# Two delays in the hand-written weaving of a recurrence: the first half starts nearer the head of the products, its first steps lie closer

## The chip, the cores and the metric

The kernel runs on one core of one Trainium2 chip. The metric is the device time of one execution in microseconds, as the median of several runs. One execution was also profiled; the times "in the trace" are those of that one execution, counted from its start.

## The reference, cut to what matters

The program has two layers over 1024 tokens with a width of 2048 (16 heads of 128). Only layer one, a gated linear recurrence (HGRN2), is touched by the change:

```
q, fz, i, g = split(h @ w_in, 4)
logf = log(lb + (1 - lb) * sigmoid(fz));  k = (1 - lb) * sigmoid(-fz);  v = i
b = cumsum(logf)  (in chunks)
o_t = q_t . S_t,   S_t = diag(f_t) S_{t-1} + k_t^T v_t          (per head)
out = (rms(o) * silu(g)) @ w_out
```

The recurrence is done in chunks: inside a chunk as a small masked attention of `q*exp(b)` with `k*exp(-b)`, between chunks by a state of 128 x 128 per head. Layer two (attention with a forget gate) follows and stays as it was.

## The kernel before, in words

Layer one is worked off in eight pairs of heads (`p` = 0 to 7). Per pair there are four big products with float32 split into two parts (three matmuls for each piece of 128 rows, called a k below): `v` (`gemm_N`, moving tiles of 256 columns), `g`, then `f` and `q` (`gemm_T`, 512 columns, eight k of three matmuls, so 24 matmuls for one head and one token half). `f` and `q` run twice, for token half `th` = 0 and then `th` = 1: f of head j=0, f of j=1, q of j=0, q of j=1.

The recurrence of one half of one pair is a generator, `hg_half`. Its steps are `hg_att` for each head (scores on TensorE, masked on VectorE by L503, and the transposition of k, copied by ScalarE in L507), `hg_state` for both heads (products on TensorE, then the state chain on VectorE: L523 for the first chunk, L525 for three more), `hg_out` for each head (seven or eight fp32 products into the tile `oa`, then square L540, sum L542, an rsqrt in small steps L221 to L227, scaling L544), and `hg_turn` for each head (four transposes of the result, a copy L552, gate L553, stores of 64 KB through SP).

What each engine executes is fixed when the program is built. The order on TensorE is written by class `Weave`: it chains all matmuls in the order in which Python emits them. `Weave` keeps a clock of its own, which only counts: `PE.tick(0.65)` after each k of a `gemm_T` and 0.33 after a k of `gemm_N`. A generator that was spawned with a delay takes its next step at the first tick after it is due; the number that it yields is the delay to its next step. `PE.need(mark)` forces steps out early when later code depends on them. The order on the other engines follows from the order in which the operations are recorded, with a scheduler that may move them.

The forget gate `hg_forget` runs for each head and half as soon as its f product is done. On ScalarE it needs a table load and two sigmoids (L470, L471), a table load and a logarithm (L472), and, after VectorE has made a running sum (L473) and small columns from it (L479 to L483), a table load and exponentials (L487, `dl` in L484, L485, L486). GpSimd scales k (L474). The decay column `dl` is kept in a dictionary that the state step reads when it is recorded:

```
        u["dl"] = dl                                            # end of hg_forget
...
        kT, st, dl = c128(u["kT"]), c128(u["S"]), u["dl"]       # hg_state
...
                    V.scalar_tensor_tensor(st[:, (n + 1) % 4, :], st[:, n, :], dl[:, 4 + n:5 + n],
                                           pu[:, n * P:(n + 1) * P], ALU.mult, ALU.add)
```

So the state steps L525 of a head use the `dl` of whichever forget gate of that head was recorded last before them.

The split of the next pair's weights into two parts (`split_w`: the high part by ScalarE in L232, the rest by GpSimd in L233, two pieces of 128x1024 each) lies in the same stretch: once between f and q of the second half (next `v` weights) and once after q (next `g` weights).

Of the kernel before, what the change touches and what calls it, by code (L numbers as in the profile page):

```python
# [82 lines left out]
def hybrid_trunk_kernel(ctx: ExitStack, tc: tile.TileContext, x, c, mod_w, mod_b, norm_g, a_w_in,  # L83
# [4 lines left out]
    PE = Weave(tc, nc.tensor)  # L88
# [32 lines left out]
    def ar(b, off, n, dt=F32):  # L121

        return pr(place.get(b, b), off, n, dt)
# [4 lines left out]
    def mm_ps():  # L128
        return psp.tile([P, 512], F32, tag="mm", name="mm", bufs=3)
# [118 lines left out]
    def raw_next():  # L248

        while not raws["ready"]:  # L250
            raw_load()
        return raws["ready"].pop(0)
# [12 lines left out]
    def mod_sum(*todo):  # L265

        for rb, acc in todo:
            V.tensor_scalar(acc, rawk(rb, 0), csil[:, 0:1], None, ALU.mult)
        for k in range(1, KT):
            for rb, acc in todo:  # L270
                V.scalar_tensor_tensor(acc, rawk(rb, k), csil[:, k:k + 1], acc, ALU.mult, ALU.add)  # L271
# [18 lines left out]
    def split_w(eng=None, more=True):  # L290

        rb = raw_next()
        i = wn[0] % 2
        wn[0] += 1
        for q in range(2):
            halves(eng or G, ar(8 + 2 * i, 1024 * q, 1024, F32R), ar(9 + 2 * i, 1024 * q, 1024, F32R),
                   ar(rb, 1024 * q, 1024))
        if more:
            raw_load()
        return (lambda k: ar(8 + 2 * i, k * 256, 256, F32R)), (lambda k: ar(9 + 2 * i, k * 256, 256, F32R))  # L300
# [8 lines left out]
    def gemm_T(ps, w, j, th):  # L309

        for k in range(KT):
            gemm_Tk(ps, w, j, th, k)
            PE.tick(0.65)
# [8 lines left out]
    def gemm_N(ps, w, t):  # L322

        for u in range(2):
            for k in range(KT):
                gemm_Nk(ps[:, u * 256:(u + 1) * 256], w, t + u, k)
                PE.tick(0.33)
# [165 lines left out]
    def hg_att(j):  # L493

        u = us[j]
        pa, pk = c128(sm_ps()), sm_ps()
        ks, qd, kst = c128(u["ks"]), c128(u["qd"]), c128(u["kst"])
        for n in range(4):
            PE.matmul(pa[0:64, n, :], lhsT=ks[:, n, 0:64], rhs=qd[:, n, :], start=True, stop=True)
            PE.matmul(pa[64:P, n, 64:P], lhsT=ks[:, n, 64:P], rhs=qd[:, n, 64:P], start=True, stop=True)  # L500
        for rows, cs in ((slice(0, 64), slice(0, P)), (slice(64, P), slice(64, P))):
            m = keep[rows, cs]
            V.copy_predicated(u["att"][rows, :, cs],  # L503
                              m.rearrange("p (o q) -> p o q", o=1).broadcast_to([64, 4, m.shape[1]]), pa[rows, :, cs])
        for n in range(4):
            PE.transpose(pk[:, n * P:(n + 1) * P], kst[:, n, :], ident)
        S.activation(u["kT"], pk, AF.Copy)  # L507

    def hg_state(j, th, v):

        u = us[j]
        pu = sm_ps()
        kT, st, dl = c128(u["kT"]), c128(u["S"]), u["dl"]
        js = slice(j * P, (j + 1) * P)
        nl = 3 if th == 1 else 4
        for n in range(nl):
            PE.matmul(pu[:, n * P:(n + 1) * P], lhsT=kT[:, n, :], rhs=v(th * 4 + n)[:, js], start=True, stop=True)
        with tc.high_priority():
            if th == 1:
                V.tensor_scalar(st[:, 0, :], st[:, 0, :], dl[:, 0:1], None, ALU.mult)  # L520
            for n in range(nl):
                if th == 0 and n == 0:
                    V.tensor_copy(st[:, 1, :], pu[:, 0:P])  # L523
                else:
                    V.scalar_tensor_tensor(st[:, (n + 1) % 4, :], st[:, n, :], dl[:, 4 + n:5 + n],  # L525
                                           pu[:, n * P:(n + 1) * P], ALU.mult, ALU.add)

    def hg_out(h, j, th, v):
        u = us[j]
        po = oa_ps()  # L530
        pov = c128(po)
        att, qd, st = u["att"], c128(u["qd"]), c128(u["S"])
        js = slice(j * P, (j + 1) * P)
        for n in range(4):
            first = th == 0 and n == 0
            PE.matmul(pov[:, n, :], lhsT=att[:, n, :], rhs=v(th * 4 + n)[:, js], start=True, stop=first)
            if not first:
                PE.matmul(pov[:, n, :], lhsT=qd[:, n, :], rhs=st[:, n, :], start=False, stop=True)
        sq = u["sq"]
        S.activation(sq, po, AF.Square)  # L540
        ss = sml.tile([P, 4], F32, name="ss")
        V.tensor_reduce(ss, c128(sq), AX.X, ALU.add)  # L542
        r = rsqrt_mean(ss, 4, 1.0 / P)
        V.tensor_tensor(c128(sq), pov, spread(r, 4, P), ALU.mult)  # L544

    def hg_turn(h, j, th, sg):

        u = us[j]
        pg = sm_ps()
        for n in range(4):  # L550
            PE.transpose(pg[:, n * P:(n + 1) * P], u["sq"][:, n * P:(n + 1) * P], ident)
        S.activation(u["ogT"], pg, AF.Copy, scale=ongc[:, h:h + 1])  # L552
        G.tensor_tensor(u["ogT"], u["ogT"], sg(j, th), ALU.mult)  # L553
        for n in range(4):
            dma(ogd[th * 4 + n][:, h, :], u["ogT"][:, n * P:(n + 1) * P])

    def hg_half(p, th, v, sg):
        for j in range(2):
            hg_att(j)
            PE.marks.add(("att", p, j, th))  # L560
            yield 4.5
        if p > 0 or th == 1:
            PE.need(("out", p - 1 + th, 1, 1 - th))
        for j in range(2):
            hg_state(j, th, v)
        yield 4.0
        if p > 0 or th == 1:
            PE.need(("half", p - 1 + th, 1 - th))
        for j in range(2):
            hg_out(2 * p + j, j, th, v)  # L570
            PE.marks.add(("out", p, j, th))
            yield 5.0
        yield 2.0
        for j in range(2):
            hg_turn(2 * p + j, j, th, sg)
            yield 3.0
        PE.marks.add(("half", p, th))

    def hg_pair(p, wv, wg):
        bv, bg = 14 + (p % 2) * 2, 15 + (p % 2) * 2  # L580

        def v(t):
            return ar(bv, t * 256, 256)

        def sg(j, th):
            return ar(bg, j * 1024 + th * 512, 512)

        def put_v(ps, t):
            S.activation(ar(bv, t * 256, 512), ps, AF.Copy)

        def put_g(ps, j, th):
            S.activation(sg(j, th), ps, AF.Sigmoid)
            V.tensor_tensor(sg(j, th), ps, sg(j, th), ALU.mult)

        if p == 0:
            for t in range(0, NT, 2):
                put_v(vps[t // 2], t)
            for j in range(2):
                put_g(gps[j], j, 0)
        else:  # L600
            for t in range(0, NT, 2):
                ps = mm_ps()
                gemm_N(ps, wv, t)
                put_v(ps, t)
        wf = split_w()
        for th in range(1 if p == 0 else 0, 2):
            for j in range(2):
                ps = mm_ps()
                gemm_T(ps, wg, j, th)
                put_g(ps, j, th)  # L610
        wq = split_w()

        for i in range(3):
            mod_sum((raw_next(), accs[i]))
            raw_load()
            PE.spawn(mod_later(mods_left.pop(0), accs[i]), 15.0 + 5.0 * i)
        for th in range(2):
            if th == 1:
                PE.spawn(hg_half(p, 0, v, sg), 5.0)
            for j in range(2):  # L620
                ps = mm_ps()
                gemm_T(ps, wf, j, th)
                if p > 0 or th == 1:
                    PE.need(("att", p - 1 + th, j, 1 - th))
                hg_forget(2 * p + j, us[j], ps)
            if th == 1:
                nwv = split_w() if p + 1 < NP else None
            for j in range(2):
                ps = mm_ps()
                gemm_T(ps, wq, j, th)  # L630
                if p > 0 or th == 1:
                    PE.need(("out", p - 1 + th, j, 1 - th))
                V.tensor_tensor(us[j]["qd"], ps, us[j]["eb"], ALU.mult)
        nwg = split_w() if p + 1 < NP else None
        PE.spawn(hg_half(p, 1, v, sg), 5.0)
        return nwv, nwg

    def mod_later(b, acc):
        mod_cols(b, acc, sm_ps()[:, 0:256])
        PE.marks.add(("mod", b))  # L640
        yield 0.0

    for p in range(NP):
        wv, wg = hg_pair(p, wv, wg)
# [737 lines left out]
```

## Time and profile before

| | |
|---|---|
| median of 3 runs | 2374.51 us (2373.2 to 2376.35) |
| profiled execution, its own time | 2370.9 us |
| its span in the trace | 2369.2 us |
| TensorE (PE) busy | 2263.2 us, 96% |
| VectorE (DVE) / ScalarE (ACT) / GpSimd (POOL) busy | 63% / 43% / 25% |

How to read it: PE is busy nearly all the time, so the time can only fall where PE is idle or runs at the lower clock, and it rises where a new idle stretch opens on PE. Idle time of the other engines costs nothing by itself.

### The profile page before, as it was taken

How to read it: one execution, taken by the hardware profiler on the slowest of the kernel's cores; microseconds unless marked ns; L12 is line 12 of the kernel's file. 1: busy time of each engine (PE TensorE's matmuls, PEld its weight loads, DVE VectorE, ACT ScalarE, POOL GpSimd, SP SyncE). 2: the span in 40 equal slices, each digit the busy share in tenths (PEclk: the TensorE clock that was granted, in tenths of full speed). 3: DMA queues.
4: the chain of work that ended last, by engine and by line, in shares of the span. 5: the costliest groups of instructions: out<-in, count | busy, mean ns of one | idle time of the engine just before them, and what ended most of it. 6: DMA issues, size and time to landing. Idle time of an engine off the chain costs nothing.

```text
span 2369.2 us, 38021 instructions
## 1 busy us (share of the span) xinstructions
PE 2263.2 (96%) x14376; PEld 2026.4 (86%) x14376; DVE 1501.3 (63%) x3838; ACT 1016.6 (43%) x1634; POOL 601.9 (25%) x514
## 2 busy tenths in 40 slices
PE   4999999999999999999798999999999999999999
PEld 3888888888888798788688999989999999998887
DVE  7565555665656566646867547667767766777533
ACT  5454444444353536324323324444544544455321
POOL 3222222221222221101332222433343334333000
PEclk9999999999999999999899999999999999999999
DMA  8313131313132223565322323512222222235443
GB/s 272 102 41 103 45 98 46 98 54 98 55 89 72 72 85 95 189 217 182 106 90 81 124 86 99 177 57 68 88 74 73 88 78 84 68 94 175 154 145 115
DMA packets 220315, 245.18 MB, mean 103 GB/s; under 512 B 14610, under 2 KB 182964, under 8 KB 220132
## 3 DMA queue, kind: packets, MB, share of 16 engines
q1 hardware_dynamic: 220132, 242.75, 32.8%
q8 instruction: 113, 1.85, 0.3%
q14 instruction: 70, 0.57, 0.1%
HBM read 196.36 MB, written 46.34 MB: 102 GB/s over the span
## 4 chain that ended last, share of the span: by engine, by line
PE 73%; DVE 11%; ACT 6%; issue 4%; DMA 4%; POOL 1%; SPq 0%; ACTq 0%; DVEq 0%; POOLq 0%
PE mm L48 53%; PE oa L48 8%; PE sm L48 7%; PE sm L51 5%; DVE blk L233 2%; DVE blk L271 1%; DVE dl L479 1%; ACT blk L232 1%; DVE blk L473 1%; ACT L472 1%; DMA blk<-in_mod_w_dram 1%; ACT L487 1%; ACT blk L472 1%; POOL blk L233 1%; ACT L470 1%
## 5 line engine op out<-in xcount | busy, mean ns | idle before, releaser
L48 PE MATMUL mm<-blk,blk 128*128 128x512 f32 (+1 forms) x9120 | 1726.0, 343 | 15.2 <-DVE blk L233 7.9
L48 PEld LDWEIGHTS mm<-blk,blk 128*128 128x128 f32 x9120 | 1419.5, 192 | 185.9 <-DVE blk L233 10.5
L232 ACT ACTIVATE blk<-blk 128x1024 fp32r<-128x1024 f32 (+3 forms) x372 | 335.4, 914 | 461.2 <-PE mm L48 281.1
L233 DVE TENSOR_TENSOR blk<-blk,blk 128x1024 fp32r<-128x1024 f32 (+3 forms) x268 | 276.2, 1039 | 228.8 <-ACT blk L232 225.2
L233 POOL TENSOR_TENSOR blk<-blk,blk 128x1024 fp32r<-128x1024 f32 (+1 forms) x104 | 240.0, 2314 | 308.6 <-ACT blk L232 302.5
L48 PE MATMUL oa<-blk,blk 128*128 128x256 f32 (+1 forms) x2016 | 286.4, 287 | 27.8 <-DVE blk L523 14.7
L48 PEld LDWEIGHTS oa<-blk,blk 128*128 128x128 f32 x2016 | 267.4, 196 | 39.2 <-DVE blk L523 16.0
L48 PE MATMUL sm<-blk,blk 128*128 128x256 f32 (+6 forms) x1824 | 269.2, 303 | 0.1
L48 PEld LDWEIGHTS sm<-blk,blk 128*128 128x128 f32 (+2 forms) x1824 | 218.2, 175 | 23.2 <-issue 3.5
L51 PE MATMUL sm<-ident,blk 128*128 128x128 f32 x1201 | 187.8, 277 | 36.2 <-DVE blk L931 12.6
L51 PEld LDWEIGHTS sm<-ident,blk 128*128 128x128 f32 x1201 | 144.6, 142 | 63.3 <-issue 32.0
L1226 ACT ACTIVATE blk<-blk,m 128x128 f32<-128x128 f32 (+7 forms) x128 | 99.0, 773 | 127.5 <-DVE m L1224 117.4
L233 DVE TENSOR_TENSOR blk<-sm,blk 128x512 fp32r<-128x512 f32 (+1 forms) x160 | 92.9, 581 | 62.7 <-ACT blk L232 62.2
L1228 POOL TENSOR_SCALAR blk<-blk,smx 128x128 f32<-128x128 f32 (+7 forms) x128 | 98.1, 767 | 135.6 <-DVE smx L1227 121.2
L271 DVE SCALAR_TENSOR_TENSOR blk<-blk,cc,blk 128x256 f32<-128x256 f32 x196 | 111.2, 570 | 20.6 <-DMA blk<-in_mod_w_dram 13.8
L1198 POOL TENSOR_TENSOR blk<-rows4k,keep 128x128 f32<-128x128 f32 x128 | 63.0, 492 | 226.8 <-DVE mx L1205 208.4
L553 POOL TENSOR_TENSOR blk<-blk,blk 128x512 f32<-128x512 f32 x32 | 42.5, 1327 | 238.4 <-ACT blk L552 238.4
L232 ACT ACTIVATE blk<-sm 128x512 fp32r<-128x512 f32 (+1 forms) x160 | 81.1, 507 | 48.7 <-PE sm L51 47.9
L1205 DVE CUSTOM_DVE_ANT_0 blk<-sm,rows4k 128x128 f32<-128x128 f32 (+3 forms) x176 | 84.6, 494 | 22.9 <-PE sm L48 21.4
L474 POOL TENSOR_SCALAR blk<-blk,cc 128x512 f32<-128x512 f32 x32 | 22.9, 716 | 260.7 <-ACT blk L471 257.4
L487 ACT ACT_TABLE_LOAD x31 | 39.8, 1283 | 103.0 <-DVE blk L482 103.0
L473 DVE TENSOR_TENSOR_SCAN blk<-rows4k,blk 128x512 f32<-128x512 f32 x32 | 39.1, 1223 | 70.3 <-ACT blk L472 70.3
(167 smaller groups left out, 1776.2 us busy)
## 6 DMA issues: line engine op xcount, KB each, us to landing
blk<-in_a_w_in_dram SPq DMA_DIRECT2D x64, 512.0 KB, 3.9
blk<-in_mod_w_dram SPq DMA_DIRECT2D x48, 512.0 KB, 4.7
blk<-in_kv_w_dram SPq DMA_DIRECT2D x32, 512.0 KB, 4.1
blk<-in_b_w_in_dram SPq DMA_DIRECT2D x32, 512.0 KB, 3.9
ogd<-blk SPq DMA_DIRECT2D x128, 64.0 KB, 1.9
blk<-in_kv_mod_w_dram SPq DMA_DIRECT2D x16, 512.0 KB, 3.5
blk<-in_a_w_out_dram SPq DMA_DIRECT2D x16, 512.0 KB, 3.9
blk<-ogd SPq DMA_DIRECT2D x16, 512.0 KB, 3.8
```

The costliest lines, as they stand in the source:

```text
L48: self._chain(self.PE.matmul(*a, **k))
L51: self._chain(self.PE.transpose(*a, **k))
L232: S.activation(hi, src, AF.Copy)
L233: eng.tensor_tensor(lo, src, hi.bitcast(F32), ALU.subtract)
L271: V.scalar_tensor_tensor(acc, rawk(rb, k), csil[:, k:k + 1], acc, ALU.mult, ALU.add)
L472: S.activation(u["lf"], u["lf"], AF.Ln, bias=lc, scale=oc)
L473: V.tensor_tensor_scan(u["b"], rst, u["lf"], 0.0, ALU.mult, ALU.add)
L487: S.activation(lf[:, :, 1, :], lf[:, :, 1, :], AF.Exp)
L1198: G.tensor_tensor(nfm, nF[:, i * P:n], negm, ALU.add)
L1205: V.tensor_tensor_reduce(dst, src, add, 1.0, -3e38, ALU.add, ALU.max, mx[:, nm:nm + 1])
L1226: S.activation(l[:, 0:n], l[:, 0:n], AF.Exp, bias=m, accum_out=sm)
L1228: G.tensor_scalar(l[:, 0:n], l[:, 0:n], sm, 0.0, ALU.mult, ALU.add)
```

## The change

Two numbers. The delay with which the first half's `hg_half` is spawned at the start of the second half's f product goes from 5.0 to 1.0, and the delay after each `hg_att` from 4.5 to 3.5 (that one holds for both halves of every pair).

```
@@ -558,7 +558,7 @@
         for j in range(2):
             hg_att(j)
             PE.marks.add(("att", p, j, th))
-            yield 4.5
+            yield 3.5
         if p > 0 or th == 1:
             PE.need(("out", p - 1 + th, 1, 1 - th))
         for j in range(2):
@@ -616,7 +616,7 @@
             PE.spawn(mod_later(mods_left.pop(0), accs[i]), 15.0 + 5.0 * i)
         for th in range(2):
             if th == 1:
-                PE.spawn(hg_half(p, 0, v, sg), 5.0)
+                PE.spawn(hg_half(p, 0, v, sg), 1.0)
             for j in range(2):
                 ps = mm_ps()
                 gemm_T(ps, wf, j, th)
```

The order on TensorE (PE), first pair, at the head of the second half's f product of head 0. The `mm` rows are that product, the `sm` rows with 64x128 and 64x64 are `hg_att` of head 0, L51 its transposes.

```order
 L48 MATMUL mm<-blk_0_77,blk_0_87 128x512
+L48 MATMUL sm<-blk_0_111,blk_0_109 64x128
+L48 MATMUL sm<-blk_0_111,blk_0_109 64x64
+L48 MATMUL sm<-blk_0_111,blk_0_109 64x128
+L48 MATMUL sm<-blk_0_111,blk_0_109 64x64
+L48 MATMUL sm<-blk_0_111,blk_0_109 64x128
+L48 MATMUL sm<-blk_0_111,blk_0_109 64x64
+L48 MATMUL sm<-blk_0_111,blk_0_109 64x128
+L48 MATMUL sm<-blk_0_111,blk_0_109 64x64
+L51 MATMUL sm<-ident,blk_1_110 128x128 x4
 L48 MATMUL mm<-blk_0_79,blk_0_85 128x512
 L48 MATMUL mm<-blk_1_80,blk_0_85 128x512
```

The step stands now behind 2 of the 8 k of that product; before it stood behind all 8. Counted on PE in the same way for every pair but the last (there the output projection follows in place of the next v product): `hg_att` of head 1 moves from behind 7 k of f of head 1 to behind 7 k of f of head 0; `hg_state` from behind 6 k of q of head 0 to behind 5 k of f of head 1; `hg_out` of head 0 from behind the whole of q of head 0 to behind its first 3 k; `hg_out` of head 1 from behind the whole of q of head 1 to behind its first 3 k; `hg_turn` of head 0 from behind 84 matmuls of the next pair's v product to behind 30, that of head 1 from behind 111 to behind 57.

The order on ScalarE (ACT), third pair, from behind the logarithm of head 0's second half to that of head 1. First before; the two L232 are the pieces of the next v weights, L484 is `dl`, L507 the copy of `hg_att` of head 1.

```order
L232 ACTIVATE blk_0_85<-blk_0_93 128x1024
L487 ACT_TABLE_LOAD
L487 ACTIVATE blk_0_105<-blk_0_105 128x4x64
L484 ACTIVATE dl<-dl 128x8
L485 ACTIVATE blk_1_108<-blk_0_107 128x512
L486 ACTIVATE blk_0_109<-blk_0_107 128x512
L507 ACTIVATE blk_0_113<-sm 128x512
L470 ACT_TABLE_LOAD
L470 ACTIVATE blk_0_105<-mm 128x512
L471 ACTIVATE blk_1_106<-mm 128x512
L472 ACT_TABLE_LOAD
L472 ACTIVATE blk_0_105<-blk_0_105,cc 128x512
```

And the same place of the changed kernel:

```order
L232 ACTIVATE blk_0_85<-blk_0_93 128x1024
L487 ACT_TABLE_LOAD
L487 ACTIVATE blk_0_105<-blk_0_105 128x4x64
L232 ACTIVATE blk_1_86<-blk_1_94 128x1024
L484 ACTIVATE dl<-dl 128x8
L485 ACTIVATE blk_1_108<-blk_0_107 128x512
L486 ACTIVATE blk_0_109<-blk_0_107 128x512
L470 ACT_TABLE_LOAD
L470 ACTIVATE blk_0_105<-mm 128x512
L471 ACTIVATE blk_1_106<-mm 128x512
L472 ACT_TABLE_LOAD
L472 ACTIVATE blk_0_105<-blk_0_105,cc 128x512
```

The second weight piece has moved in front of `dl`, and the L507 has gone: it stands now ahead of the first sigmoid table load of head 0, with that of `hg_att` of head 0.

The order on VectorE (DVE), third pair, at the rsqrt of the first half's head 0, up to L544, for which `hg_turn` of head 0 waits. Before:

```order
L222 TENSOR_SCALAR rs_t<-rs_m 128x4
L223 TENSOR_SCALAR rs_y<-rs_t 128x4
L225 SCALAR_TENSOR_TENSOR rs_t<-rs_y 128x4
L226 TENSOR_TENSOR rs_t<-rs_t,rs_m 128x4
L227 SCALAR_TENSOR_TENSOR rs_y<-rs_t,rs_y 128x4
L225 SCALAR_TENSOR_TENSOR rs_t<-rs_y 128x4
L226 TENSOR_TENSOR rs_t<-rs_t,rs_m 128x4
L227 SCALAR_TENSOR_TENSOR rs_y<-rs_t,rs_y 128x4
L225 SCALAR_TENSOR_TENSOR rs_t<-rs_y 128x4
L226 TENSOR_TENSOR rs_t<-rs_t,rs_m 128x4
L227 SCALAR_TENSOR_TENSOR rs_y<-rs_t,rs_y 128x4
L544 TENSOR_TENSOR blk_1_112<-oa,rs_y 128x512
```

And the changed kernel:

```order
L226 TENSOR_TENSOR rs_t<-rs_t,rs_m 128x4
L542 TENSOR_REDUCE ss<-blk_1_112 128x4
L490 TENSOR_TENSOR blk_1_110<-blk_0_109,dl 128x4x64
L227 SCALAR_TENSOR_TENSOR rs_y<-rs_t,rs_y 128x4
L221 TENSOR_SCALAR rs_m<-ss 128x4
L225 SCALAR_TENSOR_TENSOR rs_t<-rs_y 128x4
L222 TENSOR_SCALAR rs_t<-rs_m 128x4
L226 TENSOR_TENSOR rs_t<-rs_t,rs_m 128x4
L223 TENSOR_SCALAR rs_y<-rs_t 128x4
L227 SCALAR_TENSOR_TENSOR rs_y<-rs_t,rs_y 128x4
L225 SCALAR_TENSOR_TENSOR rs_t<-rs_y 128x4
L544 TENSOR_TENSOR blk_1_112<-oa,rs_y 128x512
```

Head 0's rsqrt stands no longer by itself: ahead of its end come L542 of head 1 (which needs `hg_out` of head 1 and its square L540) and the last step of the forget gate, L490, and the steps of the two rsqrts alternate.

## Rows read from the trace of the kernel before

**Rows 1.** The page: busy time of each engine, share of the span, instructions.

```profile
PE 2263.2 (96%) x14376; PEld 2026.4 (86%) x14376; DVE 1501.3 (63%) x3838; ACT 1016.6 (43%) x1634; POOL 601.9 (25%) x514
```

**Rows 2.** Waits of PE, 100 to 1180 us: waiting line, waited for, total us, times, longest.

```profile
PE oa L48 <- DVE blk L523: 14.7, 7, 2.1
PE oa L48 <- DVE blk L525: 9.8, 7, 1.5
```

**Rows 3.** Timeline of PE, third pair (last row: fifth): start, length, what, [idle <- releaser].

```profile
347.90 5.74 PE L48 MATMUL mm<-blk,blk 128*128 128x512 f32 x24
...
354.49 1.09 PE L48 MATMUL sm<-blk,blk 128*64 128x128 f32 x16
355.50 0.65 PE L51 MATMUL sm<-ident,blk 128*128 128x128 f32 x4
...
370.35 0.60 PE L48 MATMUL oa<-blk,blk 128*128 128x128 f32 x4
373.05 0.71 PE L48 MATMUL oa<-blk,blk 128*128 128x128 f32 x4 [2.10 <-DVE blk L523]
375.23 1.65 PE L48 MATMUL oa<-blk,blk 128*128 128x128 f32 x6 [1.47 <-DVE blk L525]
...
382.90 1.72 PE L48 MATMUL oa<-blk,blk 128*128 128x128 f32 x14
384.38 5.99 PE L48 MATMUL mm<-blk,blk 128*128 128x256 f32 x48
...
396.11 0.60 PE L51 MATMUL sm<-ident,blk 128*128 128x128 f32 x4
...
600.76 1.65 PE L48 MATMUL oa<-blk,blk 128*128 128x128 f32 x6 [1.48 <-DVE blk L525]
```

**Rows 4.** Windows: stretch, length, busy PE, PEld, DVE, ACT, POOL, clock, DMA, GB/s.

```profile
378.00:379.00 1.00, 1.00 (x5) 0.85 (x4) 0.72 (x3) 1.00 (x4) 0.00 (x0) 0.86 0.06 19
...
606.00:607.00 1.00, 1.00 (x4) 0.75 (x3) 1.00 (x4) 0.00 (x0) 0.00 (x0) 0.52 0.00 0
```

**Rows 5.** Timeline of ACT, third pair, forget gate of head 1, second half.

```profile
366.31 0.58 ACT L507 ACTIVATE blk<-sm 128x512 f32<-128x512 f32 x1
366.91 1.28 ACT L470 ACT_TABLE_LOAD   x1
...
370.60 0.81 ACT L472 ACTIVATE blk<-blk,cc 128x512 f32<-128x512 f32 x1
371.32 1.04 ACT L232 ACTIVATE blk<-blk 128x1024 fp32r<-128x1024 f32 x1
376.43 1.28 ACT L487 ACT_TABLE_LOAD   x1 [4.06 <-DVE blk L482]
...
378.66 0.62 ACT L486 ACTIVATE blk<-blk 128x512 f32<-128x512 f32 x1
```

**Rows 6.** Timeline of DVE, the same stretch.

```profile
371.45 1.23 DVE L473 TENSOR_TENSOR_SCAN blk<-rows4k,blk 128x512 f32<-128x512 f32 x1 [3.25 <-ACT blk L472]
372.70 0.29 DVE L523 COPY blk<-sm 128x128 f32<-128x128 f32 x1
372.91 1.95 DVE L479 COPY dl<-blk 128x4 f32<-128x4 f32 x1
...
375.93 0.42 DVE L482 TENSOR_TENSOR blk<-dl,blk 128x256 f32<-128x256 f32 x1
...
381.21 0.68 DVE L542 TENSOR_REDUCE ss<-blk 128x4 f32<-128x512 f32 x1
...
384.20 2.28 DVE L225 SCALAR_TENSOR_TENSOR rs_t<-rs_y 128x4 f32<-128x4 f32 x1
...
388.08 0.69 DVE L544 TENSOR_TENSOR blk<-oa,rs_y 128x512 f32<-128x512 f32 x1
```

**Rows 7.** Timeline of POOL, the same stretch.

```profile
372.50 2.34 POOL L233 TENSOR_TENSOR blk<-blk,blk 128x1024 fp32r<-128x1024 f32 x1 [2.42 <-ACT blk L232]
...
384.06 2.40 POOL L233 TENSOR_TENSOR blk<-blk,blk 128x1024 fp32r<-128x1024 f32 x1 [0.33 <-ACT blk L232]
```

More of the change, by code (lines that the diff above doesn't have):

```diff
@@ L560, in hg_half @@
             PE.marks.add(("att", p, j, th))
-            yield 4.5
+            yield 3.5
         if p > 0 or th == 1:
@@ L618, in hg_pair @@
             if th == 1:
-                PE.spawn(hg_half(p, 0, v, sg), 5.0)
+                PE.spawn(hg_half(p, 0, v, sg), 1.0)
             for j in range(2):
```

## The prediction, written before the changed kernel was run

> **What bounds the kernel now.** I read the page first: PE is busy 96% of the span [rows 1], so only its gaps and its clock can give time back. The list of waits of PE then names nearly all of layer one's gaps: in the tile `oa`, 7 times for L523 and 7 times for L525, 24.5 us in all [rows 2]; one of the eight pairs has none. The timeline of the third pair shows the place: `hg_out` of head 0 starts at 370.35, stands 2.10 us for the first chunk's state and 1.47 us for the next [rows 3]. The reader should see that VectorE is late there: L523 runs only at 372.70, behind the running sum of head 1's gate, and a long L479 stands between it and the first L525 [rows 6].
>
> What one such stop costs: from the start of `hg_out` of head 0 to that of head 1 there are 12.55 us [rows 3], for 14 short rows (1.48, from 382.90 to 384.38) and 24 products of 0.24 us (the row at 347.90), together 7.2. So 5.3 us are lost: 3.57 idle, 1.5 by the clock, which the windows show at half (1.2 GHz) until 378.3, 3.0 us after PE ran again, and 0.3 by refilling. In two pairs it stays low about twice as long (in the fifth PE runs again at 600.76 and the clock is back at 607.0 [rows 3, 4], the sixth is alike), which costs some 1.6 us more each. Mean loss 5.8 us, in seven pairs 41 us.
>
> **The change, part by part.** No instruction is added in number on PE, no byte is moved more; the eight stores of `hg_turn` go out earlier on SP and nobody waits for them before the next `hg_turn`. Everything is order. I walk the third pair on the clock of its rows, as if the changed order had run there from 347.90 on.
>
> *PE up to hg_out.* 15 products fewer stand ahead of it (q's last 5 k): 370.35 - 15 x 0.24 = 366.75. `hg_att` of head 1 starts at 354.49 - 0.7 + 1.5 = 355.3 (one k fewer ahead, head 0's step more) and its transposes end 1.66 later [rows 3], at 356.95.
>
> *The forget gate of head 0.* ScalarE must first copy those transposes (0.58), and only then comes the sigmoid's table load: from 357.5 the load, two sigmoids, load and logarithm take 4.50 us (366.91 to 371.41 [rows 5]): 362.0. In the old order that load lay hidden ahead of the product. The weight piece L232 follows (to 362.95), and GpSimd's L233 from 363.1 to 365.45. The running sum ends at 363.25, L523 of head 1 at 363.5, and then L479 meets L233. What that costs the rows show: L479, of 4 columns, started at 372.91 and ended at 374.86, GpSimd's L233 at 374.84 [rows 6, 7]. So L479 ends at 365.45, L482 about 1.0 later (1.49 before, with one L525 and one L523 more between) at 366.45, the exponential of L487 1.7 later at 368.2. Now the second L232 (0.95) stands ahead of `dl`: 369.3, first L525 369.65.
>
> *hg_out of head 0* can pass four products (0.85) until 367.6 and then waits for that L525, because it reads the `dl` of the second half: about 2.0 us idle in place of 3.57. Had the state read its own `dl`, there would be none.
>
> *Down the same chain to hg_turn.* This is what nobody waited for before: `hg_turn` stood at 396.11, 7 us behind the end of L544 (388.77). ScalarE goes on: L485, L486 until 370.3 (2.85 from load to L486, plus L232), the 4.50 us of head 1: 374.8. Running sum to 376.1, L542 to 376.75, some 1.5 for four short steps, q's product with the exponential and L482: 378.2. Table load to L486 2.85: 381.1. Square L540 of head 1, taken as the 0.58 of L507: 381.65. The next L232 ends at 382.6 and GpSimd holds from 382.75 to 385.15 and, 0.33 behind, from 385.5 to 387.9 [rows 5, 7]. VectorE ends L542 of head 1 at about 382.5 and has then nine operations with all operands in SBUF ahead of L544. L225 of 4 columns took 2.28 us, until GpSimd ended [rows 6, 7]; L523, with its input in PSUM, ran 0.29 in the midst of a L233. So I take the nine as held, but for two in the gap, and L525 and L544 as free. Behind 387.9 some seven remain, at 0.1 to 0.2 us each (386.48 to 388.08 is eight in a row, 0.2 each; two alternating chains may go closer): 389.0, and L544 ends at 389.7.
>
> The Trainium skill ("GPSIMD Engine Reference", section Specifications) says that GpSimd shares its SBUF interfaces with VectorE and contends with VectorE instructions that run in a two-port mode or have two SBUF inputs. By that rule L490 and the rsqrt's steps wait too and the time stays at the 2404 us below; without such contention it would be the first rival's 2359. The two holds in this trace agree (1.95 and 2.28 us).
>
> PE is at `hg_turn` sooner: from 366.75 on 1.48 + 39 x 0.24 + 1.48 + 30 x 0.125 (the row at 384.38) = 16.1 makes 382.8 without any stop. So PE loses 389.7 - 382.8 = 6.9 us up to there, however it is split: about 2.3 in `hg_out`, 4.6 at `hg_turn`. A slower clock after the first stop is only swallowed by the second.
>
> *Behind it.* All later products of PE are queued behind these transposes. There are 0.3 us of refilling, and the low clock: after the old stops it stayed low for 3.0 to 6.2 us of running, 1.5 to 3.1 us lost [rows 3, 4]. For a single stop of 4.6 us I take 2.0, bounds 0 and 3.1. `hg_turn` of head 1 waits for nothing: its L544 comes some 3 us behind the first, PE needs 5 to reach it. Loss per pair 9.2 against 5.8: +3.4, in seven pairs +24 us.
>
> *The other half's 1 us.* `hg_att` of head 1 to `hg_state` is 33 products of 0.125, 4 us, and `hg_state` to `hg_out` 36 as before; before it caused no stop, so nothing.
>
> *Last pair.* It had no stop. There are no weights to split by GpSimd, but `dl` falls behind further table loads, and the output projection's own splits lie on VectorE ahead of L544. Bounds 0 and the 9.2 of the others; nearer the second, since the gate's chain is the same: 6.
>
> Sum: 2370.9 + 24 + 6 = 2401 for an execution like the profiled one; the median of the runs lies 3.6 above that, so 2404 us.
>
> **The rivals.** *No hold (faster).* If the nine operations slip past GpSimd, L544 ends at 382.5 + 1.5 + 0.7 = 384.8. Then PE, delayed by 2.3 in `hg_out` to 385.1, does not stop a second time; loss 2.3 and perhaps 0.8 of clock, 3.1 against 5.8: -19 us, last pair +3: 2359. It decides at one point, whether L544 is ready by 385. For it speaks that many VectorE steps run beside GpSimd unharmed; against it the two held rows, and that the split follows L540 by rule of the order, so it comes along when the chain moves.
>
> *It does what it seems to do.* Both stops vanish, -41 us: 2334. It needs `dl` 2 us earlier and L544 7 us earlier; only if ScalarE's chain were much shorter than its rows.
>
> *One hold.* Only the first L233 is met: L544 at 387.3, loss 4.5 + 0.3 + 1.5 = 6.3, +4 in seven pairs and +6 in the last: 2384.
>
> **Chances.** My forecast 0.68, one hold 0.15, no hold 0.12, all vanishes 0.05. Range: downwards to the case of one hold and, since its last pair may cost nothing and the clock less, to 2374; upwards 3.1 in place of 2.0 of clock (+8), a chain 1 us longer (+7) and the whole 9.2 in the last pair (+3): 2422. Differences within 0.2% (4.7 us) count as the same. Faster: the last two cases less a remnant, 0.16; the same: 0.06, from the light end of one hold; slower 0.78.
>
> **What would show it.** In the changed kernel: PE's waits in `oa` for L523 gone, one for L525 of about 2 us in seven pairs; a new wait of L51 into `sm` for L544 of 3 to 5 us, 30 products into the next pair; L490 or an rsqrt step of over 2 us beside L233 ahead of it; the clock at half right behind that wait and not so much behind `hg_out`. Wrong if there is no wait for L544: then one of the two holds or ScalarE's chain was shorter than its rows. Wrong in size if the clock stays up, or if the waits in `oa` are over 3 us, which would say that L525 is held too.

## The result, and the profile after

| kernel | median | range | runs |
|---|---|---|---|
| before, beside it | 2373.86 us | 2371.86 to 2376.35 | 4 |
| changed | 2391.16 us | 2388.95 to 2393.48 | 4 |

The changed kernel is slower: ratio 1.0072, 95% interval 1.0055 to 1.009, or +17.3 us. The profiled execution took 2390.87 us over a span of 2389.2 us. The prediction was 2404 us: right in sign and in the place of the loss, 13 us too high.

The page of the changed kernel, busy time by engine (answers to [rows 1]):

```profile
PE 2264.1 (95%) x14376; PEld 2027.6 (85%) x14376; DVE 1471.2 (62%) x3838; ACT 1017.7 (43%) x1636; POOL 603.5 (25%) x514
```

PE does the same work in the same busy time; of the 20 us more of span 19 are idle time of PE (125.1 us against 106.0). Its list of waits from 100 to 1200 us (answers to [rows 2]): waiting line, waited for, total us, times, longest.

```profile
PE oa L48 <- DVE blk L525: 18.2, 8, 2.6
PE sm L51 <- DVE rs_t L226: 18.1, 6, 3.8
...
PE sm L51 <- issue: 2.2, 1, 2.2
```

The waits for L523 are gone, as forecast. One wait for L525 is left in each pair, now also in the last. The second and third rows are new: `hg_turn`'s transposes (L51 into `sm`), in all seven pairs that are followed by another. The list names L226 because that was running last; the rows on VectorE below show that the data come from L544 (the tile that L51 reads). The timeline of PE in the third pair (answers to [rows 3]):

```profile
370.53 1.05 PE L48 MATMUL oa<-blk,blk 128*128 128x128 f32 x8
373.81 1.50 PE L48 MATMUL oa<-blk,blk 128*128 128x128 f32 x6 [2.22 <-DVE blk L525]
374.96 6.88 PE L48 MATMUL mm<-blk,blk 128*128 128x512 f32 x24
381.67 1.72 PE L48 MATMUL oa<-blk,blk 128*128 128x128 f32 x14
383.15 7.29 PE L48 MATMUL mm<-blk,blk 128*128 128x512 f32 x45
392.64 0.63 PE L51 MATMUL sm<-ident,blk 128*128 128x128 f32 x4 [2.20 <-DVE rs_t L226]
```

From the start of `hg_out` at 370.53 to `hg_turn` at 392.64 there are 22.1 us for 16.1 us of work: 6.0 lost. What ended each wait is read on VectorE (answers to [rows 6]):

```profile
367.39 2.12 DVE L479 COPY dl<-blk 128x4 f32<-128x4 f32 x1
...
373.40 1.11 DVE L525 SCALAR_TENSOR_TENSOR blk<-blk,dl,sm 128x128 f32<-128x128 f32 x3 [0.55 <-ACT dl L484]
...
385.74 0.68 DVE L542 TENSOR_REDUCE ss<-blk 128x4 f32<-128x512 f32 x1
...
386.67 2.37 DVE L227 SCALAR_TENSOR_TENSOR rs_y<-rs_t,rs_y 128x4 f32<-128x4 f32 x1
...
389.07 2.30 DVE L225 SCALAR_TENSOR_TENSOR rs_t<-rs_y 128x4 f32<-128x4 f32 x1
...
391.80 0.69 DVE L544 TENSOR_TENSOR blk<-oa,rs_y 128x512 f32<-128x512 f32 x1
```

And on GpSimd (answers to [rows 7]):

```profile
366.94 2.54 POOL L233 TENSOR_TENSOR blk<-blk,blk 128x1024 fp32r<-128x1024 f32 x1 [2.42 <-ACT blk L232]
...
386.47 4.88 POOL L233 TENSOR_TENSOR blk<-blk,blk 128x1024 fp32r<-128x1024 f32 x2 [8.88 <-ACT blk L232]
```

Three steps of four columns, L479, L227 and L225, take 2.12 to 2.37 us each, and each ends with a L233. L544 ends at 392.49, and PE runs 0.15 later.

### The profile page after: what moved, and what is told of

Read it like the earlier page. It is cut to its first block, busy times and chain, and to the rows that moved or that the text cites. A ratio compares the mean times of both kernels' runs of the same rounds, so it can differ in the third digit from the quotient of the medians.

```text
span 2389.2 us, 38021 instructions
## 1 busy us (share of the span) xinstructions
PE 2264.1 (95%) x14376; PEld 2027.6 (85%) x14376; DVE 1471.2 (62%) x3838; ACT 1017.7 (43%) x1636; POOL 603.5 (25%) x514
## 4 chain that ended last, share of the span: by engine, by line
PE 46%; DVE 6%; issue 3%; DMA 2%; POOL 1%; ACT 1%; SPq 0%; DVEq 0%; ACTq 0%; POOLq 0%
PE mm L48 31%; PE oa L48 6%; PE sm L48 5%; PE sm L51 4%; DVE blk L233 2%; ACT blk L232 1%; DMA blk<-xnd 1%; DMA blk<-in_b_w_out_dram 0%; DVE rs_t L225 0%; POOL blk L1059 0%; DVE blk L847 0%; DVE rs_t L222 0%; DVE blk L952 0%; DVE blk L851 0%; DVE ss L928 0%
## 5 line engine op out<-in xcount | busy, mean ns | idle before, releaser
L232 ACT ACTIVATE blk<-blk 128x1024 fp32r<-128x1024 f32 (+3 forms) x372 | 335.8, 913 | 461.5 <-PE mm L48 287.2
L233 DVE TENSOR_TENSOR blk<-blk,blk 128x1024 fp32r<-128x1024 f32 (+3 forms) x268 | 279.2, 1049 | 236.9 <-ACT blk L232 231.8
L233 POOL TENSOR_TENSOR blk<-blk,blk 128x1024 fp32r<-128x1024 f32 (+1 forms) x104 | 241.1, 2328 | 403.2 <-ACT blk L232 363.9
L48 PE MATMUL oa<-blk,blk 128*128 128x256 f32 (+1 forms) x2016 | 282.8, 286 | 20.9 <-DVE blk L525 18.2
L51 PE MATMUL sm<-ident,blk 128*128 128x128 f32 x1201 | 188.2, 278 | 57.1 <-DVE rs_t L226 18.1
L51 PEld LDWEIGHTS sm<-ident,blk 128*128 128x128 f32 x1201 | 144.4, 142 | 85.0 <-issue 54.4
L233 DVE TENSOR_TENSOR blk<-sm,blk 128x512 fp32r<-128x512 f32 (+1 forms) x160 | 93.0, 581 | 62.3 <-ACT blk L232 61.7
L232 ACT ACTIVATE blk<-sm 128x512 fp32r<-128x512 f32 (+1 forms) x160 | 81.0, 506 | 48.9 <-PE sm L51 48.1
L1205 DVE CUSTOM_DVE_ANT_0 blk<-sm,rows4k 128x128 f32<-128x128 f32 (+3 forms) x176 | 84.6, 494 | 23.0 <-PE sm L48 20.9
L553 POOL TENSOR_TENSOR blk<-blk,blk 128x512 f32<-128x512 f32 x32 | 42.3, 1320 | 167.9 <-ACT blk L552 162.8
L227 DVE SCALAR_TENSOR_TENSOR rs_y<-rs_t,rs_y 128x4 f32<-128x4 f32 (+2 forms) x270 | 64.9, 241 | 5.4
```

The costliest lines, as they stand in the source:

```text
L48: self._chain(self.PE.matmul(*a, **k))
L51: self._chain(self.PE.transpose(*a, **k))
L227: V.scalar_tensor_tensor(y, t, 1.5, y, ALU.add, ALU.mult)
L232: S.activation(hi, src, AF.Copy)
L233: eng.tensor_tensor(lo, src, hi.bitcast(F32), ALU.subtract)
L1205: V.tensor_tensor_reduce(dst, src, add, 1.0, -3e38, ALU.add, ALU.max, mx[:, nm:nm + 1])
```

## The experiments

All are timed in four runs, beside seven runs of the kernel before on the same chip (2373.5, 2370.64 and 2374.71 us in the three sets). The ratio is to those.

| kernel | median | ratio, 95% interval |
|---|---|---|
| delay of 1.0 alone | 2335.98 us | 0.9844, 0.9828 to 0.9861 |
| yield of 3.5 alone | 2352.26 us | 0.991, 0.9895 to 0.9925 |
| changed, `hg_turn` later | 2362.99 us | 0.995, 0.9935 to 0.9965 |
| changed, g split recorded later | 2392.16 us | 1.0081, 1.0066 to 1.0096 |
| changed, own `dl` | 2386.45 us | 1.0058, 1.0042 to 1.0075 |
| changed, own `dl`, `hg_turn` later | 2336.97 us | 0.9854, 0.9839 to 0.9869 |
| changed, g split behind `hg_turn` | 2361.65 us | 0.9958, 0.9943 to 0.9973 |
| delay of 3.0, yield of 3.5 | 2347.96 us | 0.9899, 0.9882 to 0.9915 |
| the same, g split behind `hg_turn` | 2330.0 us | 0.9815, 0.9799 to 0.9832 |
| changed, own `dl`, g split behind `hg_turn` | 2343.94 us | 0.9875, 0.986 to 0.9889 |

The theory was the prediction's: two results come late, `dl` of the other half for L525 and L544 for `hg_turn`, and L544 is late in part because of two holds beside GpSimd's L233. Its rivals: one of the two numbers is bad by itself; the stop at `hg_out` is what costs; ScalarE's chain is late and the long steps on VectorE only hide a wait; the early places on TensorE cost something in themselves.

**Each number alone.** First the delay, with the yield put back (all diffs are against the changed kernel):

```
-            yield 3.5
+            yield 4.5
```

> The changed kernel with the yield behind hg_att put back to 4.5; only the delay of 1.0 stays. In the order on TensorE hg_state then stands behind all 8 k of f of head 1, hg_out of head 0 behind 6 k of q of head 0 (9 products later than in the changed kernel), hg_turn of head 0 behind 48 short products and the second half's first hg_att. Theory (two late results, dl of the second half for the first L525 and L544 for hg_turn, each measured against the place of the step that waits): PE comes 9 x 0.24 = 2.2 us later to hg_out, so the 2.2 us stop there shrinks to under 0.5 us; PE comes some 3.9 us later to hg_turn, which was 5.9 us late in all, so about 2 us stay there. Loss per pair 2 to 4 us against 7.5 of the changed kernel: 2355 to 2370 us. Rival 'the delay of 1.0 is the whole cost': as the changed kernel, 2389 to 2393. Rival 'the shorter yield is the whole cost': as the kernel before, 2374.

Measured: 2335.98 us, 38 us faster than before and 19 us below the range expected. Between 100 and 1160 us there is no wait for L523 or L525, and of `hg_turn` only two short ones:

```profile
PE sm L51 <- DVE blk L544: 1.2, 2, 0.8
```

Both single-cause rivals fall. What the expectation missed is in VectorE's queue:

```profile
355.29 1.63 DVE L525 SCALAR_TENSOR_TENSOR blk<-blk,dl,sm 128x128 f32<-128x128 f32 x6
...
358.36 1.23 DVE L473 TENSOR_TENSOR_SCAN blk<-rows4k,blk 128x512 f32<-128x512 f32 x1 [1.24 <-ACT blk L472]
...
373.55 0.69 DVE L544 TENSOR_TENSOR blk<-oa,rs_y 128x512 f32<-128x512 f32 x1
```

Here all six L525 stand ahead of the running sum L473 of head 1's gate, so `hg_out` waits for nothing, and L544 ends 15.9 us behind the start of `hg_out` (358.37 to 374.24) where the changed kernel needs 22.0. L222 and L225 are held there too and take 1.79 and 2.34 us, but PE comes to `hg_turn` behind that.

Then the yield, with the delay put back:

```
-                PE.spawn(hg_half(p, 0, v, sg), 1.0)
+                PE.spawn(hg_half(p, 0, v, sg), 5.0)
```

> The changed kernel with the spawn delay put back to 5.0; only the shorter yield of 3.5 stays. hg_state moves from behind 6 k to behind 3 k of q of head 0, hg_out stays where it was before (behind the whole q), hg_turn of head 0 stands 18 short products earlier (2.25 us) than before. On VectorE the first half's L523 and three L525 then stand ahead of the running sum of head 1's gate. Theory: with that the stop for L523 and that for the first L525 in hg_out both vanish, and hg_turn, which had 7 us to spare before, has no wait or one under 1 us: loss per pair 0 to 1 us against 5.8 before, 2333 to 2345 us, faster than both kernels. Rival 'the shorter yield is the whole cost of the change': 2389 to 2393. Rival 'the delay of 1.0 is the whole cost, the yield does nothing': 2374.

Measured: 2352.26 us, faster than before, 7 us above the range expected. Both stops at `hg_out` are gone and `hg_turn` of head 0 waits for nothing, as the theory said. Its waits show what was not foreseen:

```profile
PE sm L51 <- DVE blk L503: 11.0, 7, 1.9
...
PE sm L48 <- ACT blk L507: 5.2, 7, 0.7
```

The yield also moves the second half's two `hg_att` together, and L503 of the first of them lies on VectorE behind L544 of head 1; and `hg_state` of head 1 comes ahead of its L507. Seven times 2.3 us is the 16 us by which this kernel lies above the delay alone.

So each number alone gains, 38 and 21 us, and both together lose 17.

**Where the loss sits.** `hg_turn` is moved back behind the late L544:

```
-        yield 2.0
+        yield 8.0 if th == 0 else 2.0
```

> The changed kernel with the yield ahead of hg_turn 8.0 in place of 2.0 for the first half: hg_turn of head 0 stands some 66 matmuls later (about 9 us), all else in the same order. Theory: the wait for L544 vanishes (it was 2.2 to 3.8 us), what stays is the stop of 2.2 us at hg_out and in some pairs 1.6 us of low clock behind it; loss 2.3 to 3.9 per pair against 7.5: 2355 to 2368 us. Rival 'the low clock and the stop at hg_out are the cost, L544 is only where the time is booked': less than 8 us better, 2383 to 2391.

Measured: 2362.99 us, inside the theory's range; the wait of `hg_turn` is gone, the eight for L525 are unchanged (18.2 us). The rival that the wait is only where another loss is booked falls.

Then the other wait alone is taken away: each state step keeps its own half's `dl`.

```
     def hg_att(j):
         u = us[j]
+        u["own"] = u["dl"]
...
-        kT, st, dl = c128(u["kT"]), c128(u["S"]), u["dl"]
+        kT, st, dl = c128(u["kT"]), c128(u["S"]), u["own"]
```

> The changed kernel, but each state step reads the dl of its own half (kept when hg_att is recorded), so that the first L525 waits for no later forget gate; TensorE's order is the same. Theory (what decides is when L544 comes, and that hangs on the forget gate of head 1 and two L233, not on hg_out): the 2.2 us stop at hg_out vanishes, and PE stands at hg_turn by as much longer, 5 to 6.5 us in place of 2.2 to 3.8; 2385 to 2398 us, the changed kernel's 2391 within 7. Rival 'the stop at hg_out is worth its idle time': 7 x 2.2 + 2.6 = 18 us better, 2373, or 2360 with the low clock gone as well.

Measured: 2386.45 us, and the wait moved. There is no stop at `hg_out`, and PE stands at `hg_turn` for 4.7 us in six pairs and 4.2 in the first (5 to 6.5 were expected). PE in the third pair:

```profile
371.70 1.72 PE L48 MATMUL oa<-blk,blk 128*128 128x128 f32 x14
373.18 5.74 PE L48 MATMUL mm<-blk,blk 128*128 128x512 f32 x24
...
392.23 1.09 PE L51 MATMUL sm<-ident,blk 128*128 128x128 f32 x4 [4.71 <-DVE rs_t L226]
```

`hg_out` now takes its 1.48 us without a gap, the next 24 products run at full clock, and the time comes back to within 5 us of the changed kernel's. The rival by which this stop is worth its idle time (2373 or less) falls. (The scheduler also gave ScalarE and VectorE another order in this kernel: from the start of `hg_out` L544 ends after 20.4 us where the changed kernel needs 22.0. That is why the wait is shorter than expected.)

The edit also changes what is computed. In the reference a chunk's state decays by the chunk's own tokens. The changed kernel (for head 0 of each pair) and the kernel before (for both heads) read `u["dl"]` when the second half's gate has already replaced it, and apply the second half's decay to the first half's states. So the wait for that `dl` is not one that the recurrence asks for. Every kernel here that leaves the state step as it was computes this too, the fastest included.

With both edits:

> The changed kernel with both: state steps that read their own half's dl, and the yield ahead of the first half's hg_turn at 8.0 in place of 2.0. Theory: both stops of TensorE are gone, the clock stays at its full level between them, and the whole loss of 7.5 us per pair comes back: 2332 to 2342 us, as the kernel with the delay of 1.0 alone (2336). Rival 'something else than the two stops also makes the changed kernel slow': above 2350.

Measured: 2336.97 us, in the theory's range, with no wait of PE for the recurrence over 0.7 us. The two stops and the clock behind them are the whole loss.

**Are the holds real?** A first try recorded the split of the next g weights two tiles later, in the next pair's v product:

```
+                if t == 2:
+                    wg = split_w()
...
-        nwg = split_w() if p + 1 < NP else None
```

> The changed kernel with the split of the next g weights (two L232 on ScalarE, two L233 on GpSimd) recorded inside the next pair's v product, behind its second tile, and not at the end of the pair. TensorE's order is the same. Theory (the two rsqrt steps L227 and L225 stand 2.37 and 2.30 us beside these two L233): without them L544 comes about 4.4 us earlier, PE at hg_turn of head 0 waits 0 to 1 us, no step L221 to L227 takes over 0.3 us there: 2355 to 2370 us. Rival 'the chain from ScalarE is late by itself and the two long steps only hide a wait': hg_turn still waits 2 to 4 us, 2385 to 2393.

Measured: 2392.16 us, which looks like the rival. It is not evidence: the scheduler put both L232 and both L233 back to their old places (L233 at 385.06 to 389.90 with L227 at 2.36 and L225 at 2.26 us beside it), so it only times the changed kernel a second time. The second try ties the order (`turned` holds the last L553 recorded):

```
-        eng.tensor_tensor(lo, src, hi.bitcast(F32), ALU.subtract)
+        ins = eng.tensor_tensor(lo, src, hi.bitcast(F32), ALU.subtract)
+        if behind:
+            tc.add_manual_dep(ins.ins, behind[0].ins.name,
+                              mybir.DependencyInfo(mybir.DependencyClass.NoSync, mybir.DependencyReason.DATA),
+                              reason="split behind hg_turn")
...
+        turned[:] = [G.tensor_tensor(u["ogT"], u["ogT"], sg(j, th), ALU.mult)]
...
+                if t == 2:
+                    behind[:] = turned
+                    wg = split_w()
+                    behind[:] = []
...
-        nwg = split_w() if p + 1 < NP else None
```

> The changed kernel with the two L233 of the next g weights put behind L553 of the first half's hg_turn in GpSimd's queue by a dependency of order, recorded in the next pair's v product. TensorE's and VectorE's orders stay the same; ScalarE's part of the split stays where it was. (The earlier try recorded the split later, and the scheduler put it back to the same place.) Theory (GpSimd's two L233 hold L227 and L225 by 2.37 and 2.30 us): those two take under 0.5 us, L544 ends some 4.5 us earlier, TensorE comes to hg_turn 0 to 1 us ahead of it, and the stop at hg_out stays: 2355 to 2370 us. Rival 'the chain behind ScalarE is late by itself': the wait at hg_turn stays at 2 us or more, 2383 or above.

Measured: 2361.65 us, in the theory's range. VectorE in the third pair, in VectorE's unchanged order (this kernel has more lines: L548 is the changed kernel's L542, L550 its L544, L531 its L525, L489 its L483 and L235 its L233):

```profile
378.20 0.68 DVE L548 TENSOR_REDUCE ss<-blk 128x4 f32<-128x512 f32 x1
...
379.13 0.16 DVE L227 SCALAR_TENSOR_TENSOR rs_y<-rs_t,rs_y 128x4 f32<-128x4 f32 x1
...
379.32 0.16 DVE L225 SCALAR_TENSOR_TENSOR rs_t<-rs_y 128x4 f32<-128x4 f32 x1
...
379.91 0.69 DVE L550 TENSOR_TENSOR blk<-oa,rs_y 128x512 f32<-128x512 f32 x1
```

PE there:

```profile
366.26 0.94 PE L48 MATMUL oa<-blk,blk 128*128 128x128 f32 x6 [2.22 <-DVE blk L531]
...
382.72 0.60 PE L51 MATMUL sm<-ident,blk 128*128 128x128 f32 x4
```

The same L227 and L225 take 0.16 us each. From the start of the reduction to the end of L544 it is 2.4 us where the changed kernel needs 6.75. L544 is ready at 380.60, 2.1 us before PE comes. Without the holds there is no wait at `hg_turn`.

Then the own `dl` and this split together, with TensorE's order left as in the changed kernel:

> The changed kernel with TensorE's order untouched, but state steps that read their own half's dl, and the two L233 of the next g weights behind L553 of hg_turn. Theory (the loss of the changed kernel is the wait for the other half's dl and the two holds beside L233, and nothing else): no stop at hg_out; L544 ends about 388.1 on the clock of the kernel with own dl, TensorE is at hg_turn at 387.5, so 0 to 0.6 us of wait stay there; 2335 to 2345 us. Rival 'the early places on TensorE cost by themselves': above 2352.

Measured: 2343.94 us, in the theory's range, 47 us under the changed kernel. At `hg_out` there is no stop, at `hg_turn` one of 0.9 us:

```profile
PE sm L51 <- DVE rs_t L226: 5.4, 6, 0.9
```

So the early places on TensorE cost next to nothing by themselves; the late results do.

**Place or number?**

```
-                PE.spawn(hg_half(p, 0, v, sg), 1.0)
+                PE.spawn(hg_half(p, 0, v, sg), 3.0)
```

> The changed kernel with a spawn delay of 3.0 in place of 1.0; the yield stays 3.5. In the order, hg_state (behind all 8 k of f of head 1), hg_out (behind 6 k of q of head 0) and hg_turn of head 0 stand where they stand in the kernel with the delay of 1.0 and the yield of 4.5 (2336 us), and VectorE's order is that one's too; only hg_att stands elsewhere. Theory 'the places of hg_state, hg_out and hg_turn against the forget gate of head 1 decide, not either number': 2333 to 2342 us. Rival 'the effect grows with the shortening of the delay': between the 2352 of the yield alone and 2391, about 2370.

Measured: 2347.96 us, 6 us above the theory's range and far below the rival's value. `hg_state`, `hg_out` and `hg_turn` of head 0 and VectorE's order are those of the delay alone, and still 12 us are lost, as waits of 1.1 to 1.5 us of `hg_turn` for L544. The two traces part at one place. VectorE with the delay of 3.0:

```profile
352.33 1.21 DVE L503 COPY_PREDICATED blk<-keep,sm 64x512 f32<-64x512 int32 x2 [2.50 <-PE sm L48]
353.57 1.23 DVE L473 TENSOR_TENSOR_SCAN blk<-rows4k,blk 128x512 f32<-128x512 f32 x1
...
355.16 0.42 DVE L482 TENSOR_TENSOR blk<-dl,blk 128x256 f32<-128x256 f32 x1
355.50 2.60 DVE L483 TENSOR_TENSOR blk<-blk,dl 128x256 f32<-128x256 f32 x1
```

GpSimd of the same kernel:

```profile
355.25 2.57 POOL L233 TENSOR_TENSOR blk<-blk,blk 128x1024 fp32r<-128x1024 f32 x1 [3.48 <-DVE dl L481]
```

With the delay of 1.0 alone, VectorE and then GpSimd:

```profile
350.78 0.42 DVE L483 TENSOR_TENSOR blk<-blk,dl 128x256 f32<-128x256 f32 x1
```

```profile
350.94 2.50 POOL L233 TENSOR_TENSOR blk<-blk,blk 128x1024 fp32r<-128x1024 f32 x1 [3.46 <-DVE blk L482]
```

In the one kernel L483 starts 0.16 us ahead of L233 and takes 0.42; in the other it comes 0.25 us behind L233's start and takes 2.60. That 0.4 us comes from L503 of `hg_att` of head 1: the logarithm of head 0's gate is done at 353.13, but its running sum L473 starts only behind L503, at 353.57. Counted from the start of `hg_out`, both L544 end 1.2 us later than with the delay alone. The theory "places decide" was too coarse: with these places the same, the rows part where one of two instructions starts first. No run moved that one start by itself. What was tested is whether the loss lies in the late L544 or in the other place of `hg_att`: the g split was put behind `hg_turn` here too, by the same dependency:

> The kernel with the delay of 3.0 (2348 us), with the two L233 of the next g weights put behind L553 of the first half's hg_turn in GpSimd's queue. Theory (what that kernel loses against the 2336 us of the delay of 1.0 with the yield of 4.5 is a forget gate that comes 1.25 us later because L483 was caught beside a L233, and then a L544 of head 1 that comes 1.2 us late for hg_turn; with L222 and L223 no longer held by 1.78 and 2.31 us both L544 come some 4 us earlier): the 12 waits of 1.2 to 1.5 us for L544 vanish, 2333 to 2342 us. Rival 'the loss comes from the other place of hg_att on TensorE': 2345 to 2350.

Measured: 2330.0 us, 3 us under the range expected and the fastest kernel of the study: 44.7 us under the kernel before. Of the twelve waits for L544 one is left (1.2 us). L483 (here L489) is held as it was, beside the split of the next v weights; VectorE, then GpSimd:

```profile
353.25 2.60 DVE L489 TENSOR_TENSOR blk<-blk,dl 128x256 f32<-128x256 f32 x1
```

```profile
353.01 2.56 POOL L235 TENSOR_TENSOR blk<-blk,blk 128x1024 fp32r<-128x1024 f32 x1 [3.47 <-DVE dl L487]
```

So the gate is as late as without this edit, and that no longer costs anything once the rsqrt steps are free. The rival by which the place of `hg_att` costs falls.

## Why the prediction was right in sign, and where its size was off

**The stop at `hg_out`.** Right. One wait for L525 of about 2.0 us was forecast; it is 2.22 in seven pairs and 2.65 in the last. The reason given, that it reads the second half's `dl`, is shown by the kernel with its own `dl`, where there is none.

**The chain to `hg_turn`.** Right in its steps. The pair starts 3.78 us later than on the prediction's clock (370.53 for 366.75), because the pairs ahead of it have lost time. With that added, the forecast and the rows are: logarithm of head 0 365.78 and 365.86; `dl` 373.08 and 373.37; L482 of head 1 381.98 and 381.97; L486 384.88 and 384.91; L540 385.43 and 385.39; L544 393.48 and 392.49. Two holds were forecast and two came, and the split behind `hg_turn` shows that they cost what they seem to cost. (The 4.50 us that the prediction put in for head 0's gate are those of head 1's, [rows 5]; in the changed kernel both heads take 4.51.)

**The first mis-sized term: the tail of the chain.** Behind the second hold the prediction had 1.8 us to the end of L544 and 0.33 between the holds. Measured are 1.14, since the steps of the two rsqrts follow each other every 0.1 us, and no gap. So the loss up to `hg_turn` is 6.0, not 6.9.

**The second: the low clock.** 2.0 us were put behind every `hg_turn`. The windows of the changed kernel (columns as in [rows 4]) show half clock (1.2 GHz) in the second pair behind `hg_turn`, in the third pair behind `hg_out`, and full clock in the third pair behind `hg_turn`:

```profile
279.00:280.00 1.00, 1.00 (x6) 1.00 (x6) 1.00 (x1) 0.00 (x0) 1.00 (x1) 0.50 0.24 77
...
374.00:375.00 1.00, 1.00 (x7) 1.00 (x6) 0.96 (x3) 0.98 (x2) 1.00 (x1) 0.50 0.00 0
...
394.00:395.00 1.00, 1.00 (x10) 1.00 (x10) 0.93 (x3) 0.00 (x0) 0.93 (x1) 1.00 0.45 157
```

Where the clock falls at `hg_out`, PE comes later to `hg_turn`, waits 2.2 us and runs on at full clock; where it does not, PE waits 3.8 and the clock falls behind that. By the lengths of the rows behind the stops it falls once in six of the seven pairs, in the fifth at both places. So the clock was low behind `hg_out` as often as behind `hg_turn`, where the prediction had expected it behind `hg_turn` above all. Four of these eight falls are behind `hg_out` and are swallowed by the wait, as the prediction itself had said of the first stop (from `hg_out` to `hg_turn` it is 22.1 us in all seven pairs). Four are left, at 1.5 us each (from `hg_turn` to the second half's `hg_out` 20.9 us against 19.4), for which it had 2.0 in every pair.

**The sum.** The same two transposes of the modulation stand at 121.69 and 914.07 in the first and the last pair before, at 121.34 and 924.94 after: 11.2 us more in seven pairs, 1.6 each, where 3.4 was forecast (24 in all). Of the 1.8 too much, 0.9 is the tail of the chain and 1.1 the clock (2.0 against 4 x 1.5 / 7 = 0.9); that is 0.2 more than is missing, which stays open. (The 5.8 us lost per pair before are 0.1 too high: the sixth pair is not like the fifth. From `hg_out` of head 0 to that of head 1 it needs 13.3 us, the fifth 14.1.) The last pair was put at 6, with bounds 0 and 9.2. The trace is 18.4 us behind at the first transposes after it (1159.71 for 1141.27), so it cost 18.4 - 11.2 + 0.35 = 7.6: one wait of 2.65 for L525, and some more waiting of the output projection for its splits (4.5 against 1.2 us for L233, 1.3 against 2.2 for L232). PE did not wait for L544 there, so the 6 came near for other reasons than those given. The remaining 1.6 us of the 20 lie in layer two, which was not looked into.

**The rivals.** "No hold" was wrong in its premise, and the split behind `hg_turn` made it true by hand: 2361.65, where 2359 had been worked out. "One hold" did not occur: in all seven pairs two rsqrt steps of head 0 or 1 take 2.26 to 2.38 us each. "It does what it seems to do" needed `dl` 2 and L544 7 us earlier (2334); the own `dl` together with the later `hg_turn` gives 2337.

**The rule behind the holds.** The Trainium skill ("GPSIMD Engine Reference", section Specifications), which the prediction used, names VectorE instructions in a two-port mode or with two SBUF inputs as those that contend with GpSimd. The traces agree as far as they can show it: every held step had all its operands in SBUF, and L525, which reads PSUM, took 1.11 us for three beside a L233. The Trainium skill's page "SBUF — State Buffer", section SBUF: two separate sides, goes further: whichever of two such instructions starts first has the shared pair of ports for its whole length, and the other waits for its end. The trace agrees: L483 at 0.42 us when it started 0.16 ahead of L233, at 2.60 when it came 0.25 behind.

## What to carry to other kernels

Two waits on one chain are one loss: taking away the first lengthens the second, so a step on the bounding engine is worth moving only as far as the last result of its chain, and that can be forecast by walking the chain with the old rows and every engine's order (here to 0.3 us up to the square L540, to 1 us at L544). Where GpSimd works on SBUF beside VectorE, its long instructions belong behind the short VectorE steps that somebody waits for. Look in the order of the engine whether the scheduler has really moved what was moved in the code.

## What the runs showed of the hardware that was not expected

Short and long steps are held alike: beside a L233 of 2.4 to 2.6 us, L479, L225, L227 (128x4), L483 (128x256) and L222 (128x4, int32) took 1.79 to 2.60 us, L488 (128x512) 1.88 in place of 0.69 (changed kernel, at 374.44), and beside L553 (1.31 us) L226 (128x4) took 1.14 with the delay of 3.0. Not every step with all operands in SBUF is held: with the yield alone the sum L542 took its 0.67 us at 378.26, in the midst of a L233. By the rows above, a difference of 0.4 us in one start lies at the root of the 12 us between two kernels; no run shows that start by itself.

The same stop of 2.22 us at the same place lowers TensorE's clock in some pairs and not in others, with the same work ahead of it. In the kernel with `hg_turn` later, PE in the third and the fourth pair:

```profile
368.13 0.94 PE L48 MATMUL oa<-blk,blk 128*128 128x128 f32 x6 [2.23 <-DVE blk L525]
368.83 7.31 PE L48 MATMUL mm<-blk,blk 128*128 128x512 f32 x24
...
479.55 0.94 PE L48 MATMUL oa<-blk,blk 128*128 128x128 f32 x6 [2.23 <-DVE blk L525]
480.24 5.70 PE L48 MATMUL mm<-blk,blk 128*128 128x512 f32 x24
```

The 24 products take 7.31 us with the clock at half (0.50 in the windows from 369.8 to 371.8) and 5.70 at full clock. Why it falls in the one and not in the other stays open.
